# Strassen's sums built in the accumulation banks: a chain of products per bank instead of a bank per product

## The chip, the cores and the metric

The kernel runs on one core of a Trainium2 chip. The metric is the device time of one launch in microseconds, the median of the runs shown.

## What is computed

A two-layer decoder trunk on 1024 tokens of width 1024, in float32. Each sub-layer ends in `x <- LayerNorm(alpha * x + f(x))`. Layer 0 mixes with a gated linear recurrence and a convolution that share an output projection, layer 1 with pooling windows; both layers then attend to 256 memory tokens and pass a SwiGLU block of 2816 hidden channels.

```python
def memory_cross_attention(x, mem_n, w_q, w_k, w_v, w_o):
    ...
    s = jnp.einsum('bshd,bmhd->bhsm', q, k).astype(jnp.float32) * (XA_DH ** -0.5)
    p = jax.nn.softmax(s, axis=-1).astype(x.dtype)
    o = jnp.einsum('bhsm,bmhd->bshd', p, v).reshape(B, S, D_MODEL)
    return o @ w_o

def swiglu_ffn(x, w_gate, w_up, w_down):
    return (jax.nn.silu(x @ w_gate) * (x @ w_up)) @ w_down
```

## The kernel before

**Products.** A float32 product is made of three passes with float32r operands (`mm3`, lines 202 to 206): each operand is held as a high part (a cast on ScalarE, line 209) and a low part (the difference, line 210, on VectorE or GpSimd). The names `dh` and `dl` in the profile are these parts, `wp` and `raw` the loaded weights and hidden layer, `op` the parts of the gate and up stage, `D` and `P` the accumulation banks (512 floats on 128 partitions each; there are eight). A plain matmul here is 128 x 128 by 128 x 512.

**Seven products.** Most large products are taken as 2 x 2 blocks in Winograd's form of Strassen's scheme. With A in halves of its rows and of the inner dimension, and B in halves of the inner dimension and of its columns, it forms combinations S1 to S4 of A's blocks and T1 to T4 of B's, and then

```text
P1 = A11 B11   P2 = A12 B21   P3 = S4 B22   P4 = A22 T4   P5 = S1 T1   P6 = S2 T2   P7 = S3 T3
C11 = P1 + P2            C12 = P1 + P6 + P5 + P3
C21 = P1 + P6 + P7 + P4  C22 = P1 + P6 + P7 + P5
```

The function `seven` runs them for the output projection of the first mixer (once), the scores against the memory, the output of the attention (both in each layer) and the down projection (each layer). A product has four blocks of 128 tokens, each with its own bank; so a product takes four of the eight banks. It runs over pairs `g` of chunks of the inner dimension: two pairs in the attention stages (48 matmuls a product), six in the down projection, the last a single chunk (132 matmuls a product). For each pair it calls `hook` (loads, combinations, norms that are to stand there in each engine's list), prepares operands until `look(j)` pairs are ready ahead (`operands7`, through `down_B` for the weights' combinations, lines 762 to 786), and issues the matmuls for the four blocks. After a product `add` takes its four blocks. The last product of a stage goes block by block from the pair `outer` on. All engines run their lists in the order in which the program is written; a matmul waits for its bank until the tile that held it before was read for the last time.

**Sums before.** Each product starts its own banks. Sums that serve several blocks of C are made on VectorE: U = P1 + P6 (and + P7) in a tile `U` of SBUF, or several additions of the same bank to the residual rows `x` (`add_down`, `add_attn`, and `add` in the scores). In the down projection P5 and P7 are added twice per block, P6 goes into U and from there into three places, one of them on GpSimd. The orders are 1, 2, 6, 5, 3, 7, 4 in the attention stages (`ORDER_A`) and 1, 5, 7, 6, 4, 3, 2 in the down projection (`ORDER_D`).

**Gate and up.** `ffn` works on 20 pairs of chunks of the hidden layer per layer with the same scheme (order 1, 6, 2, 7, 5, 4, 3); here a product is 12 matmuls into one bank. P1 is copied to SBUF on ScalarE, and VectorE forms U2 = P1 + P6, U3 = U2 + P7 and U2 + P5 (lines 1311 to 1322); `finish` adds the last product to one of them and applies silu, or multiplies with the gate.

**Norms.** `add_res` (line 241) puts a bank on the residual; the last addition to a row half also gives the row sums (`acc`), from which `ln_a` and `ln_b` (lines 256 and 257) make the norm. In `ffn_down` the norms of blocks 4 to 7 (`norm_b`) are called in the hook of P3.

## Time and profile before

| | us |
|---|---|
| median of 3 runs (lowest, highest) | 2537.41 (2535.52, 2541.55) |
| span of the profiled execution | 2534.8 |
| time of the profiled execution | 2537.4 |
| TensorE busy | 2338.5 (92%) |
| VectorE busy | 2010.5 (79%) |
| ScalarE busy | 1009.6 (40%) |
| GpSimd busy | 1097.2 (43%) |

The span runs from the first to the last instruction of one execution. The page gives shares of the whole span; the stages differ, so the table of windows (a stretch of time, and how long each engine was busy in it) is read beside it. In a timeline row the first number is the start, the second the duration, and the brackets give how long the engine had been idle and which instruction ended the wait.

### The profile page before, as it was taken

Reading aid. Unit: us, or ns where it says so; the run is one execution under the profiler, and the core shown is the slowest. Engines: PE = TensorE matmul, PEld = TensorE weight load, DVE = VectorE, ACT = ScalarE, POOL = GpSimd, SP = SyncE. Lnnn points to the kernel's source line nnn. Section 1 sums busy time; section 2 is a strip of 40 time slices with the busy share of each in tenths; the row PEclk is TensorE's granted clock in tenths of the full one; section 3 lists DMA queues with packets and bytes.
Section 4 is the critical chain, followed back from the end, with each engine's and each line's share of the span. In section 5 each row is a group of like instructions: output and inputs, shape, how many; then the busy total and the mean of one; then the engine's idle time right before and its main releaser. Section 6 shows DMA issues by size and latency. Waiting matters only on the chain. (4 is left out here: it accounts for less than half of the span.)

```text
span 2534.8 us, 29436 instructions
## 1 busy us (share of the span) xinstructions
PE 2338.5 (92%) x11208; PEld 1927.8 (76%) x11208; DVE 2010.5 (79%) x2202; ACT 1009.6 (40%) x1647; POOL 1097.2 (43%) x601
## 2 busy tenths in 40 slices
PE   8999998898988999999887999798899999998987
PEld 6777777686867888888676789686688888876766
DVE  6986789988996777777888856899867777778777
ACT  3255554353636323223232444455552322332342
POOL 2332447776581212212754674567511121237464
PEclk9999999898999999999998999899999999999989
DMA  4211133140202323323733343202122332356332
GB/s 179 67 34 34 34 118 124 59 167 9 100 26 92 107 81 115 115 83 129 273 117 130 107 159 101 91 17 108 51 77 90 116 116 80 116 191 224 112 110 98
DMA packets 84476, 263.26 MB, mean 104 GB/s; under 512 B 8432, under 2 KB 8944, under 8 KB 84336
## 3 DMA queue, kind: packets, MB, share of 16 engines
q1 hardware_dynamic: 58464, 203.97, 23.4%
q10 hardware_dynamic: 25872, 57.42, 6.4%
q8 instruction: 88, 1.44, 0.2%
q14 instruction: 52, 0.43, 0.1%
HBM read 198.97 MB, written 62.39 MB: 103 GB/s over the span
## 5 line engine op out<-in xcount | busy, mean ns | idle before, releaser
L204 PE MATMUL D<-dh,dl 128*128 128x512 f32 x1176 | 476.2, 405 | 87.4 <-POOL dl L210 52.1
L205 PE MATMUL D<-dl,dh 128*128 128x512 f32 x1176 | 477.0, 406 | 56.4 <-DVE dl L210 56.3
L206 PE MATMUL D<-dh,dh 128*128 128x512 f32 x1176 | 472.1, 401 | 0.0
L205 PE MATMUL P<-xl,op 128*128 128x512 f32 x1120 | 435.7, 389 | 0.0
L204 PE MATMUL P<-xh,op 128*128 128x512 f32 x1120 | 435.7, 389 | 0.0
L206 PE MATMUL P<-xh,op 128*128 128x512 f32 x1120 | 435.7, 389 | 0.0
L204 PEld LDWEIGHTS D<-dh,dl 128*128 128x128 f32 x1176 | 229.9, 196 | 145.9 <-POOL dl L210 57.7
L1199 POOL TENSOR_TENSOR s<-hf,hf 128x512 f32<-128x512 f32 x22 | 35.7, 1622 | 659.4 <-PE P L206 560.8
L205 PEld LDWEIGHTS D<-dl,dh 128*128 128x128 f32 x1176 | 230.3, 196 | 117.4 <-DVE dl L210 69.7
L210 POOL TENSOR_TENSOR dl<-raw,dh 128x1024 fp32r<-128x1024 f32 x84 | 230.0, 2751 | 185.8 <-ACT dh L209 167.0
L206 PEld LDWEIGHTS D<-dh,dh 128*128 128x128 f32 x1176 | 229.7, 195 | 48.2
L205 PEld LDWEIGHTS P<-xl,op 128*128 128x128 f32 x1120 | 210.2, 188 | 43.8
L204 PEld LDWEIGHTS P<-xh,op 128*128 128x128 f32 x1120 | 210.2, 188 | 43.7
L206 PEld LDWEIGHTS P<-xh,op 128*128 128x128 f32 x1120 | 210.2, 188 | 43.5
L119 POOL TENSOR_TENSOR wl<-raw,wh 128x1024 fp32r<-128x1024 f32 x64 | 173.0, 2716 | 160.1 <-ACT wh L117 150.4
L210 DVE TENSOR_TENSOR dl<-wp,dh 128x1024 fp32r<-128x1024 f32 x96 | 172.2, 1803 | 75.5 <-ACT dh L209 65.0
L1153 DVE TENSOR_TENSOR op<-raw,op 128x512 fp32r<-128x512 f32 x200 | 151.4, 757 | 87.5 <-ACT op L1152 71.6
L1152 ACT CAST op<-raw 128x512 fp32r<-128x512 f32 x200 | 120.4, 618 | 204.8 <-DVE raw L1179 123.4
L209 ACT CAST dh<-wp 128x1024 fp32r<-128x1024 f32 x96 | 94.8, 988 | 254.4 <-DVE wp L770 65.6
L359 DVE SCALAR_TENSOR_TENSOR cacc<-sig,par,cacc 128x1023 f32<-128x1023 f32 (+14 forms) x120 | 177.5, 1479 | 2.5
L210 POOL TENSOR_TENSOR dl<-xf,dh 128x1024 fp32r<-128x1024 f32 x48 | 148.6, 3118 | 32.1 <-ACT dh L209 31.9
L210 DVE TENSOR_TENSOR dl<-B,dh 128x1024 fp32r<-128x1024 f32 x48 | 121.8, 2563 | 24.9 <-ACT dh L209 24.9
(283 smaller groups left out, 4879.1 us busy)
## 6 DMA issues: line engine op xcount, KB each, us to landing
raw<-hD SPq DMA_DIRECT2D x70, 512.0 KB, 3.4
raw<-in_wg SPq DMA_DIRECT2D x44, 512.0 KB, 3.9
raw<-in_wu SPq DMA_DIRECT2D x44, 512.0 KB, 3.3
hD<-s ACTq DMA_DIRECT2D x44, 512.0 KB, 4.8
wp<-in_wd SPq DMA_DIRECT2D x40, 512.0 KB, 5.0
xD<-x ACTq DMA_DIRECT2D x32, 512.0 KB, 4.0
x<-xD SPq DMA_DIRECT2D x32, 512.0 KB, 5.7
raw<-in_w_in SPq DMA_DIRECT2D x23, 512.0 KB, 3.4
```

The costliest lines, as they stand in the source:

```text
L119: eng.tensor_tensor(lo, raw, hi.bitcast(F32), op=ALU.subtract)
L204: mm(out, ll, rh, start=start, stop=False)
L205: mm(out, lh, rl, start=False, stop=False)
L206: mm(out, lh, rh, start=False, stop=stop)
L209: self.nc.scalar.copy(hi, src)
L210: getattr(self.nc, lo_engine).tensor_tensor(lo, src, hi.bitcast(F32), op=ALU.subtract)
L359: nc.vector.scalar_tensor_tensor(acc[:, s:], u[:, :S - s], w[:, j:j + 1], acc[:, s:], op0=ALU.mult, op1=ALU.add)
L1152: nc.scalar.copy(pg[:, 0], src)
L1153: getattr(nc, lo_engine).tensor_tensor(pg[:, 1], src, pg[:, 0].bitcast(F32), op=ALU.subtract)
L1199: gp(s1, a21, a22, op=ALU.add)
```

## The change

P6, P7 and P4 accumulate on in the four banks of P1, and P3 in those of P5 (`CHAIN`): the first matmul of such a product doesn't start the bank anew. So the banks of P1 hold P1, then P1 + P6, then P1 + P6 + P7, and last C21 complete; those of P5 hold P5, then P5 + P3. After each product of a chain its sum of so far is read where C needs it: C11 takes the bank after P1 and the bank of P2, C12 the bank after P6 and the bank after P3, C22 the bank after P7 and the bank after P5, C21 the bank after P4. The U tiles and the additions to them go. As a bank must not be written on before the sum of so far is read, the products' orders change, so that between two products of a chain another one stands, with the exception of P4 after P7 in `seven`: 1, 2, 5, 6, 3, 7, 4 (`ORDER_A`), 1, 5, 6, 3, 7, 4, 2 (`ORDER_D`), 1, 2, 6, 5, 7, 3, 4 (`ORDER_P`). With the orders some hooks move: the last combinations in the attention stages to the first pair of P6, the loads of `x` to P2 and P5, the norms of blocks 4 to 7 in the down projection from P3 to P2, and six pairs of operands are made ahead under P4 and P2 instead of P3 and P2.

```diff
+ORDER_A = (1, 2, 5, 6, 3, 7, 4)
+ORDER_D = (1, 5, 6, 3, 7, 4, 2)
+ORDER_P = (1, 2, 6, 5, 7, 3, 4)
+CHAIN = {1: 1, 6: 1, 7: 1, 4: 1, 5: 5, 3: 5, 2: 2}
+ENDS = (4, 3, 2)
...
-        def mm(bank, o, p, g):
+        def mm(bank, o, p, g, j):
             tk = slice(p * P, (p + 1) * P)
             for i in range(o[0].shape[1]):
                 c = 2 * g + i
-                self.mm3(bank, o[0][:, i, tk], o[1][:, i, tk], o[2][:, i, :], o[3][:, i, :], c == 0, c == nc - 1)
-
+                self.mm3(bank, o[0][:, i, tk], o[1][:, i, tk], o[2][:, i, :], o[3][:, i, :], c == 0 and j == CHAIN[j], c == nc - 1,
+                         j != CHAIN[j])
+
+        chains = {}
         for j in order:
-            banks = [self.ps(f"D{j}") for _ in range(4)]
             hold = []
             for g in range(ng):
                 hook(j, g)
+                if g == 0:
+                    if j == CHAIN[j]:
+                        chains[j] = [self.ps(f"D{j}") for _ in range(4)]
+                    banks = chains[CHAIN[j]]
...
-    def add_down(self, j, b, x0, x1, s0, s1, u):
...
-        elif j == 5:
-            self.add_res(x0, b, 1)
-            self.add_res(x1, b, 1)
-        elif j == 7:
-            self.add_res(x1, b, 0)
-            self.add_res(x1, b, 1, first=False)
-        elif j == 6:
-            nc.vector.tensor_tensor(u, b, u, op=ALU.add)
-            for x, eh, eng in ((x0, 1, nc.gpsimd), (x1, 0, nc.vector)):
-                sl = x[:, eh * 512:eh * 512 + 512]
-                eng.tensor_tensor(sl, sl, u, op=ALU.add)
-            self.add_res(x1, u, 1, first=False, acc=s1)
...
+    def add_block(self, j, b, x0, x1, s0, s1):
+        x, st, eh, first = {1: (x0, None, 0, True), 2: (x0, s0, 0, False), 6: (x0, None, 1, True), 3: (x0, s0, 1, False),
+                            5: (x1, None, 1, True), 7: (x1, s1, 1, False), 4: (x1, s1, 0, True)}[j]
+        self.add_res(x, b, eh, first=first, acc=st)
...
+            q, eh = {1: (p, 0), 2: (p, 0), 6: (p, 1), 3: (p, 1), 5: (p + 4, 1), 7: (p + 4, 1), 4: (p + 4, 0)}[j]
+            if j in (2, 3, 7):
+                tt(half(q, eh), b, half(q, eh), op=ALU.add)
             else:
-                tt(half(p + 4, 0), b, half(p + 4, 0), op=ALU.add)
+                nc.scalar.copy(half(q, eh), b)
...
             elif j == 7:
-                B22[g], r = take(), T3.pop(g)
-                tt(r, B22[g], r, op=ALU.subtract)
+                r = T3.pop(g)
+                tt(r, B22.pop(g), r, op=ALU.subtract)
             elif j == 6:
-                r = T[g]
+                B22[g], r = take(), T[g]
                 tt(r, B22[g], r, op=ALU.subtract)
...
-            b = self.ps(f"P{j}")
-            product(b, w, X[j])
+            if j == CHAIN[j]:
+                banks[j] = self.ps(f"P{j}")
+            b = banks[CHAIN[j]]
+            product(b, w, X[j], j == CHAIN[j])
...
-            if j == 1:
-                p1 = self.t2("p1", [512])
-                nc.scalar.copy(p1, b)
-            elif j == 6:
-                u2 = self.t2("u2", [512])
-                tt(u2, b, p1, op=ALU.add)
+            if j in (1, 6, 5):
+                u[j] = self.t2("u", [512])
+                nc.scalar.copy(u[j], b)
             elif j == 2:
-                finish(m, st, 0, 0, p1, b)
+                finish(m, st, 0, 0, u.pop(1), b)
             elif j == 7:
-                u3 = self.t2("u3", [512])
-                tt(u3, b, u2, op=ALU.add)
-            elif j == 5:
-                finish(m, st, 1, 1, u3, b)
-                tt(u2, b, u2, op=ALU.add)
-            elif j == 4:
-                finish(m, st, 1, 0, u3, b)
+                finish(m, st, 1, 1, u.pop(5), b)
+            elif j == 3:
+                finish(m, st, 0, 1, u.pop(6), b)
             else:
-                finish(m, st, 0, 1, u2, b)
+                finish(m, st, 1, 0, None, b)
...
-            if j == 3 and 1 <= g < 5:
+            if j == 2 and 1 <= g < 5:
                 norm_b(3 + g)
 
-        self.seven(ORDER_D, self.down_made, self.down_ops, len(self.hD), HF, lambda j: 6 if j in (3, 2) else 4, add, hook, 1)
+        self.seven(ORDER_D, self.down_made, self.down_ops, len(self.hD), HF, lambda j: 6 if j in (4, 2) else 4, add, hook, 1)
```

Three places show how the lists of the engines move. The first is VectorE's list in the first down projection, before, at the end of the block of additions that follows P6 (`U` is the tile of the sums, `x` the residual, `wp` a weight block that becomes a combination, `dl` a low part):

```order
L241 SCALAR_TENSOR_TENSOR x_9719,lst_9611<-x_9719,U_9614 128x512
L846 TENSOR_TENSOR U_9614<-D_1636_10327,U_9614 128x512
L849 TENSOR_TENSOR x_9764<-x_9764,U_9614 128x512
L241 SCALAR_TENSOR_TENSOR x_9764,lst_9612<-x_9764,U_9614 128x512
L779 TENSOR_TENSOR wp_1528_9629<-wp_1660_10507,wp_1528_9629 128x1024
L210 TENSOR_TENSOR dl_10566<-wp_1528_9629,dh_10565 128x1024
```

and after, at the additions that follow P7, the product ahead of P4 (line 247 is `add_res`, 786 the combination for P4, 216 the split):

```order
L247 SCALAR_TENSOR_TENSOR x_9449,lst_9382<-x_9449,D_1383_9396 128x512
L247 SCALAR_TENSOR_TENSOR x_9489,lst_9383<-x_9489,D_1384_9397 128x512
L247 SCALAR_TENSOR_TENSOR x_9534,lst_9384<-x_9534,D_1385_9398 128x512
L786 TENSOR_TENSOR wp_1386_9399<-wp_1534_10453,wp_1386_9399 128x1024
L216 TENSOR_TENSOR dl_10496<-wp_1386_9399,dh_10495 128x1024
```

Of a product's block nothing is left but one addition from the bank, and the next combination stands right behind the fourth.

The second place is TensorE's list in the first attention output, before, in the product after P2 (which is P6), from its first block of tokens to its second, with the waits:

```order
L204 MATMUL D_947_5881<-dh_5817,dl_5814 128x512
L205 MATMUL D_947_5881<-dl_5818,dh_5813 128x512
L206 MATMUL D_947_5881<-dh_5817,dh_5813 128x512
L204 MATMUL D_948_5882<-dh_5817,dl_5814 128x512
L205 MATMUL D_948_5882<-dl_5818,dh_5813 128x512
L206 MATMUL D_948_5882<-dh_5817,dh_5813 128x512
```

and after, where the product behind P2 is P5:

```order
L210 MATMUL D_907_5813<-dh_5741,dl_5738 128x512
L211 MATMUL D_907_5813<-dl_5742,dh_5737 128x512
L212 MATMUL D_907_5813<-dh_5741,dh_5737 128x512
L210 MATMUL D_908_5814<-dh_5741,dl_5738 128x512 [waits DVE_49]
L211 MATMUL D_908_5814<-dl_5742,dh_5737 128x512
L212 MATMUL D_908_5814<-dh_5741,dh_5737 128x512
```

Every block now waits for VectorE, which must have read the block of P2 whose bank it takes.

The third place is ScalarE's list in the gate and up stage of the first layer, in one round, before (`p` is the copy of P1):

```order
L1152 CAST op_8882<-raw_8671 128x512 [waits DMAHW1_49,DMAHW0_49,DVE_49]
L1311 COPY p_1401_8900<-P_1400_8887 128x512 [waits PE_49]
L1152 CAST op_8902<-s_8822 128x512 [waits DMAHW2_49]
L1152 CAST op_8920<-raw_8671 128x512 [waits Activation_49]
L1152 CAST op_8939<-raw_8534 128x512 [waits DVE_49,Activation_49]
```

and after (`u` is the copy of a sum from a bank):

```order
L1274 COPY u_8567<-P_1264_8552 128x512 [waits PE_49]
L1112 CAST op_8570<-raw_8351 128x512 [waits DMAHW5_49,DVE_49]
L1178 ACTIVATE sg_8550<-sg_8550 128x512 [waits DVE_49]
L1112 CAST op_8589<-raw_8212 128x512 [waits DVE_49,Activation_49]
L1274 COPY u_8604<-P_1264_8552 128x512 [waits PE_49]
```

Copies of the bank's sums after P1 and after P6 now stand among the casts of the operands.

## Rows read from the trace of the kernel before

**Rows 1.** The page, engine table: busy us, share of the span, instructions.
```profile
PE 2338.5 (92%) x11208; PEld 1927.8 (76%) x11208; DVE 2010.5 (79%) x2202; ACT 1009.6 (40%) x1647; POOL 1097.2 (43%) x601
```

**Rows 2.** Waits of TensorE by releaser: us in total, times, longest us.
```profile
PE D L205 <- DVE dl L210: 56.3, 27, 12.7
PE D L204 <- POOL dl L210: 52.1, 12, 9.6
PE D L204 <- ACT dh L209: 35.2, 11, 11.1
```

**Rows 3.** Windows by stage: from:to, us, busy PE, PEld, DVE, ACT, POOL, clock, DMA.
```profile
392.00:490.00 98.00, 82.68 (x346) 66.41 (x346) 95.69 (x76) 38.07 (x51) 82.63 (x36) 0.93 0.19 67
...
833.00:1214.00 381.00, 381.00 (x1682) 315.48 (x1682) 278.31 (x399) 118.93 (x203) 71.59 (x42) 1.00 0.34 113
1214.00:1475.00 261.00, 226.37 (x926) 180.23 (x925) 217.77 (x158) 87.89 (x102) 161.66 (x71) 0.93 0.43 150
```

**Rows 4.** Windows by product of the first down projection: P7, P6, P4, P3, P2.
```profile
1292.10:1328.50 36.40, 32.88 (x134) 25.99 (x134) 28.44 (x23) 13.13 (x14) 16.47 (x7) 0.95 0.30 99
1328.50:1361.80 33.30, 30.97 (x134) 24.59 (x133) 26.59 (x21) 11.15 (x12) 15.72 (x7) 1.00 0.37 131
1361.80:1405.80 44.00, 32.52 (x133) 25.86 (x132) 37.00 (x28) 13.88 (x15) 24.31 (x12) 0.84 0.39 132
1405.80:1435.70 29.90, 29.90 (x134) 24.75 (x133) 25.01 (x21) 16.13 (x21) 23.36 (x15) 1.00 0.35 109
1435.70:1475.20 39.50, 33.67 (x135) 26.64 (x134) 32.46 (x33) 12.23 (x16) 23.41 (x12) 0.87 0.36 117
```

**Rows 5.** Timeline before and in P4, VectorE and TensorE: start, us, engine, line, [idle before].
```profile
1356.57 1.22 DVE L779 TENSOR_TENSOR wp<-wp,wp 128x1024 f32<-128x1024 f32 x1
...
1366.81 3.42 DVE L779 TENSOR_TENSOR wp<-wp,wp 128x1024 f32<-128x1024 f32 x1
1371.50 1.23 DVE L210 TENSOR_TENSOR dl<-wp,dh 128x1024 fp32r<-128x1024 f32 x1 [1.26 <-ACT dh L209]
1372.65 0.68 DVE L846 TENSOR_TENSOR U<-D,U 128x512 f32<-128x512 f32 x1
...
1373.97 1.78 DVE L241 SCALAR_TENSOR_TENSOR x<-x,U 128x512 f32<-128x512 f32 x1
...
1384.73 3.35 DVE L779 TENSOR_TENSOR wp<-wp,wp 128x1024 f32<-128x1024 f32 x1
...
1389.38 0.77 PE L204 MATMUL D<-dh,dl 128*128 128x512 f32 x1 [11.09 <-ACT dh L209]
```

**Rows 6.** Gate and up stage: one group of lines (count, busy, mean ns), two timeline rows.
```profile
L1314 DVE TENSOR_TENSOR u<-P,p 128x512 f32<-128x512 f32 x40 | 27.4, 684 | 12.4 <-PE P L206 12.4
...
1018.44 0.69 DVE L1224 TENSOR_TENSOR hf<-P,u 128x512 f32<-128x512 f32 x1 [0.79 <-PE P L206]
...
1023.08 0.69 DVE L1224 TENSOR_TENSOR hf<-P,u 128x512 f32<-128x512 f32 x1
```

**Rows 7.** Timeline in P2: first layer on TensorE, second layer on ScalarE.
```profile
1446.82 0.79 PE L205 MATMUL D<-dl,dh 128*128 128x512 f32 x1 [3.97 <-DVE dl L210]
...
2486.63 1.06 ACT L209 CAST dh<-raw 128x1024 fp32r<-128x1024 f32 x1 [8.66 <-DMA raw<-hD]
```

**Rows 8.** Timeline of the first attention output: product after P2, P2's first addition, the transposes.
```profile
714.38 0.39 PE L204 MATMUL D<-dh,dl 128*128 128x512 f32 x1
...
717.62 0.68 DVE L241 SCALAR_TENSOR_TENSOR x<-x,D 128x512 f32<-128x512 f32 x1
...
775.49 1.41 PE L266 MATMUL xt<-kc,x 128*128 128x128 f32 x8 [4.34 <-DVE U L874]
```

**Rows 9.** Timeline of the mixer output: P7's first reading, and the next stage's start.
```profile
485.57 0.68 DVE L874 TENSOR_TENSOR U<-D,U 128x512 f32<-128x512 f32 x1
...
501.42 0.58 PE L204 MATMUL pk<-wh,wl 128*128 128x256 f32 x1 [5.71 <-POOL wl L119]
```

**Rows 10.** Timeline of the first scores: the first reading of P2's sums.
```profile
592.32 0.69 DVE L1000 TENSOR_TENSOR p<-D,U 128x512 f32<-128x512 f32 x1 [6.34 <-PE D L206]
```

More of the change, by code (lines that the diff above doesn't have):

```diff
@@ L199, in drain, with mm3 @@
             self.pump()
-    def mm3(self, out, lh, ll, rh, rl, start, stop):
+    def mm3(self, out, lh, ll, rh, rl, start, stop, more=False):
         mm = self.nc.tensor.matmul
-        mm(out, ll, rh, start=start, stop=False)
-        mm(out, lh, rl, start=False, stop=False)
-        mm(out, lh, rh, start=False, stop=stop)
+        mm(out, ll, rh, start=start, stop=False, skip_group_check=more)
+        mm(out, lh, rl, start=False, stop=False, skip_group_check=more)
+        mm(out, lh, rh, start=False, stop=stop, skip_group_check=more)
     def split(self, hi, lo, src, lo_engine="vector"):
@@ L586, in mixer0_out @@
         sts = [self.sm("lst", 5) for _ in range(NT)]
-        U = [self.t2("U", [512]) for _ in range(4)]
         A, B = self.sides
@@ L596, in add @@
         def add(j, p, b):
-            self.add_attn(j, b, x[p], x[p + 4], sts[p], sts[p + 4], U[p])
+            self.add_block(j, b, x[p], x[p + 4], sts[p], sts[p + 4])
             if j == 3:
@@ L624, in hook @@
                 self.combos_B(B, 2, nc.gpsimd)
-            if j == 6:
-                load(4 + 2 * g)
-                load(5 + 2 * g)
-                if g == 1:
-                    self.combos_B(B, 3, nc.vector)
-                    self.combos_A(A, 3, nc.gpsimd)
+            if (j, g) in ((2, 1), (5, 0)):
+                load(4 + 2 * (j == 5))
+                load(5 + 2 * (j == 5))
+            if j == 6 and g == 0:
+                self.combos_B(B, 3, nc.vector)
+                self.combos_A(A, 3, nc.gpsimd)
             if j == 7:
@@ L780, in get @@
             elif j == 3:
-                r = B22.pop(g)
+                r = B22[g]
             else:
@@ L825, in seven @@
                 for p in range(4):
-                    mm(banks[p], o, p, g)
+                    mm(banks[p], o, p, g, j)
                     self.pump()
@@ L995, in add @@
         def add(j, p, b):
[L996 to L1010 removed]
+            q, eh = {1: (p, 0), 2: (p, 0), 6: (p, 1), 3: (p, 1), 5: (p + 4, 1), 7: (p + 4, 1), 4: (p + 4, 0)}[j]
+            if j in (2, 3, 7):
+                tt(half(q, eh), b, half(q, eh), op=ALU.add)
             else:
[L1012 removed]
+                nc.scalar.copy(half(q, eh), b)
         def hook(j, g):
[L1015 removed]
+            if j == 6 and g == 0:
                 self.combos_B(B, 3, nc.vector)
@@ L1082, in attn_out @@
         sts = [self.sm("lst", 6) for _ in range(NT)]
-        U = [self.t2("U", [512]) for _ in range(4)]
         self.w.lo_engine = ("gpsimd",)
@@ L1088, in add @@
                 self.ffn_first_half(layer)
-            self.add_attn(j, b, x[p], x[p + 4], sts[p], sts[p + 4], U[p])
+            self.add_block(j, b, x[p], x[p + 4], sts[p], sts[p + 4])
             if j == 3:
@@ L1106, in hook @@
                 self.combos_B(B, 2, nc.vector)
-            if j == 6:
-                for t in (4 + 2 * g, 5 + 2 * g):
+            if (j, g) in ((2, 1), (5, 0)):
+                for t in (4 + 2 * (j == 5), 5 + 2 * (j == 5)):
                     x[t] = self.page("x", [D])
                     nc.sync.dma_start(x[t], self.xD[t])
-                if g == 1:
-                    self.combos_B(B, 3, nc.vector)
-                    self.combos_A(A, 3, nc.gpsimd)
+            if j == 6 and g == 0:
+                self.combos_B(B, 3, nc.vector)
+                self.combos_A(A, 3, nc.gpsimd)
             if j in (7, 4):
@@ L1185, in operands, with product @@
                 yield operand(src[j], lo_engine)
-        def product(bank, w, x):
+        def product(bank, w, x, first):
             for k in range(4):
-                self.mm3(bank, w[k][0], w[k][1], x[k][0], x[k][1], k == 0, k == 3)
+                self.mm3(bank, w[k][0], w[k][1], x[k][0], x[k][1], k == 0 and first, k == 3, not first)
         later = self.later
@@ L1277, in ffn @@
         self.w.split_ahead = 0
-        order = (1, 6, 2, 7, 5, 4, 3)
+        order = ORDER_P
         def all_ops():
@@ L1294, in ffn @@
         self.down_made = []
+        banks, u = {}, {}
         for n, (m, j) in enumerate(stream):
@@ L1349, in ffn_down @@
         sts = [self.sm("lst", 5) for _ in range(NT)]
-        U = [self.page("U", [2, 512]) for _ in range(2)]
         gb, gx = [], []
@@ L1360, in add @@
                 norm_b(p - 1)
-            self.add_down(j, b, x[p], x[p + 4], sts[p], sts[p + 4], U[p // 2][:, p % 2, :] if U else None)
-            if j == 6 and p == 3:
-                U.clear()
+            self.add_block(j, b, x[p], x[p + 4], sts[p], sts[p + 4])
             if j == 4:
```

59 lines of the change are left out of this document (7 added, 52 removed).

## Prediction

> **What bounds the kernel now.** I read the engine table first [rows 1]: TensorE is busy for 2338.5 of 2534.8 us, so all that a change of this kind can win is the 196 us in which TensorE does nothing, plus what a lower clock costs around such gaps. The table of waits [rows 2] says who ends those gaps: the operands of the products called D, that is the splits of line 210 and the casts of line 209 (56.3 + 52.1 + 35.2 us). The windows by stage [rows 3] put them in their places: the gate and up stage (833 to 1214) has TensorE busy for 381.00 of 381.00 us at full clock. Nothing can be won there, only lost. The down projection has 226.37 of 261.00 and the mixer output 82.68 of 98.
>
> The down projection decides. Cut by product [rows 4] (132 matmuls each), P3 takes 29.90 us with TensorE busy all the time: that is the floor. P7 takes 36.4, P6 33.3, P4 44.0 and P2 39.5. These five take 183.1 us where 5 × 29.9 = 149.5 would do: 33.6 us of excess in each layer.
>
> Where P4's 14 us come from [rows 5]: VectorE makes each operand of P7, P6 and P4 by a combination (3.42 us beside GpSimd's work; 1.22 in the first row, the first of P4), ScalarE casts it, VectorE splits it (1.23): from 1366.81 to the split's end at 1372.73 about 5.85 us a pair of chunks, where TensorE needs 29.9/5.5 = 5.44. So the supply has no reserve, and whatever VectorE does in between makes TensorE's next operand late. After P6 that is the U block: from 1372.65 to 1384.73, 12.1 us for four blocks of tokens (for each, U from the bank 0.68, an addition to one x and one to the other, this with both inputs in SBUF 1.78). Only then comes the next combination, and TensorE waits 11.09 us.
>
> **The change, part by part.** *Gate and up.* Per round VectorE loses four operations (seven readings of the banks become three), ScalarE gains two copies. The removed additions cost 0.684 us each [rows 6]; a copy I put at the same, as an estimate. VectorE goes from 278 to 278 − 80 × 0.684 = 224 us a layer, ScalarE from 119 to 119 + 40 × 0.684 = 146, both of 381. TensorE is full already, so this is worth 0. The new price is a handover: P6, P7, P4 and P3 may start only when the bank's last sum has been read, 4 × 20 × 2 = 160 times. In each case one other product lies between, 12 matmuls of 381.00/1682 = 0.2265 us, so 2.72 us, against a reading of 0.68. The reader may thus come 2.0 us late for nothing. How late VectorE comes now [rows 6]: the reading at 1018.44 had waited 0.79 for its product, so it was on time; the next product ended 2.72 later, at 1021.16, and its reading stands at 1023.08, 1.9 us late. That is close, but with four operations fewer in a round it gets shorter. I take 0, from 0 to +6.
>
> *Down projection.* The U block goes: four additions after each product, about 4 × 0.68 = 2.7 us. GpSimd's additions and ScalarE's copies go with it, which were beside other work. I run the new order (P1, P5, P6, P3, P7, P4, P2) from 1292.1 on, where P5 ends; up to there all stays. P6 takes P7's place: 36.4 less the four additions of P5 that go, 2.7, makes 33.7. P3 needs no combinations: 29.9. P7's first operands are made under P3: 29.9. Under P7 VectorE has P3's additions (2.7) and, of P7 and P4, 5.5 pairs of combinations at 5.85 (32.2), together 34.9: P7's first addition comes 5 us after P7's end, and P4, the only product whose bank's last sum is the product right before it, waits for it: 5.0 + 0.7. Behind such a wait the clock is lower: P4's window of before exceeds 29.9 + 11.5 of waits by 2.6 at a granted clock of 0.84 [rows 4]; I take half, 1.3. Under P4 VectorE has 2.7 + 2.5 × 5.85 + five plain splits of 1.2 to 2.5, at most 30: no further wait. P4: 36.9. P2's splits of before stood behind the norms of four blocks, and TensorE waited 3.97 for one; in the last layer these norms also send their results out through SP's queue, in which P2's loads stood behind them: a cast waited 8.66 us for one [rows 7]. Now splits and loads come first; I give P2 31.5, for norms that end late. Sum: 33.7 + 29.9 + 29.9 + 36.9 + 31.5 = 161.9 against 183.1: **−21 us in each layer, −42 in both.** If the combinations run at 1.22 instead of 3.42, P4 has no wait: −27. If P7 is as slow as it was and the norms hold up the end by 4 more: −10.
>
> *Attention output, twice.* P7's U block goes, and with it the transposes' wait of 4.34 for it [rows 8]. Against it: all eight banks are taken when P2 ends, so P5 waits for VectorE's reading of P2. The product behind P2 started at 714.38, and the first addition of P2 ran from 717.62 to 718.30 [rows 8]: +3.9. That is −0.4; with somewhat shorter waits for splits behind it, since it starts later, −1 each; from −5 (the splits come sooner) to +5. *Mixer output.* P4 may start only after the first reading of P7, now at 485.57 behind norms; 48 matmuls of 0.2265 from 486.3 on end at 497. But the next stage has TensorE idle for 5.71 us until 501.42, for a split on GpSimd [rows 9] at the end of VectorE's and ScalarE's lists, and VectorE has 12 additions fewer. I take 0, from −3 to +6. *Scores, twice.* VectorE had waited 6.34 us for P2's sums [rows 10]: such a reading is on time. Copies on ScalarE I count like it, without a row. 0, from −1 to +3.
>
> Sum: −42 − 2 + 0 + 0 + 0 = −44. The profiled execution lies 2.6 us above its span, at 2537.4, which is the median too: **2493 us.** The good ends of all unknown costs: −54 − 10 − 3 − 2 = −69, giving 2468; the bad ends: −20 + 10 + 6 + 6 + 6 = +8, if all came at once.
>
> **Rivals.** *The banks take the place of the operands.* In the five attention stages (mixer output, two scores, two outputs) P2 to P5 and P7 to P4 are ten handovers that stand behind whatever VectorE has queued. For it: the readings at 717.62 and 485.57 were late [rows 8, 9], and VectorE is busy for 95.69 of 98 us in the mixer output. At 5 us for each it would be 50; the waits that stand elsewhere in these stages take up part of that, and with half of it, 25, the time is about 2518 (2505 to 2530). The new gaps cost clock as well: P4's window with its 11 us wait was granted 0.84 in the mean, where 1.00 is 2.4 GHz and the lower level, 1.2, is 0.50. The Trainium skill, "TensorE: Matmul & The Clock Gate", section "A second HAM failure mode: psum-queue depth-cycling", reports a kernel in which cycling through PSUM banks left small idle gaps between groups, over which the clock went up and down; by that rule this rival would be the likely one. Against it: the scores' readings are on time, and the worst gap, P4's, is counted already.
>
> *The operand chain is the bound, not what stands in it.* With 5.85 against 5.44 a pair, P6, P7 and P4 may run no faster than their combinations; what VectorE wins goes into splits that it then does earlier, for nothing. P7 and P6 stay at 36 and 33, P4 keeps a wait of 8 to 10, and the sum is −8 to 0: about 2533. The Trainium skill, "SBUF — State Buffer", section "Who interferes with whom", says that a VectorE operation with two SBUF inputs contends with GpSimd's reads and one with a single SBUF input does not; by that rule the combinations keep their 3.4 us, since GpSimd's splits stay, and only the additions get cheap. The rows agree: 0.68 from a bank, 1.78 from SBUF. Against the rival: 12.1 us of U block went with 11.09 us of waiting, nearly one for one.
>
> *Slower: the gate and up stage.* ScalarE copies three sums a round, in a queue in which a copy that waits for its product holds the casts behind it, and a cast that waits for VectorE holds the copy. The stage has no spare time, so every reading more than 2.0 us late is paid in full, 160 times. It decides from 44/160 = 0.28 us each; at 0.6 us it is +96 − 44, about 2589. For it: a reading of before was 1.9 us late. Against it: both engines are idle for a good part of each round, and VectorE has fewer readings.
>
> **How the numbers follow.** Forecast (2470 to 2508) 0.62; banks 0.18; chain 0.09; slower 0.11. The likeliest gives 2493. The range, 2470 to 2530, leaves out the slower case and most of the chain's. Faster by over 0.2% (5 us, about what a measurement of this kernel can tell from no change): 0.62 + 0.17 + 0.02 of the chain's = 0.81. Within: 0.08. Slower: 0.11.
>
> **What would show it.** In the changed profile: the wait of 11 us at P4 for line 209's cast is gone, and one of about 5 us for an addition of VectorE stands at P4's start; P3 and P7 take about 30 us, P2 about 31; in the gate and up stage TensorE is busy for 381 of 381 us and VectorE for about 224; the transposes' wait for U is gone; P5 of the attention output starts after a wait of about 4 us for an addition. If the gate and up stage is longer than 383 us, the third rival is at work; if P6 and P7 stay above 33 us, the second; if the ten handovers cost over 20 us in sum, the first.

## The result

The changed kernel takes 2483.55 us (median of 4 runs, 2480.97 to 2486.67), the kernel before in the same comparison 2537.86 (4 runs): a ratio of 0.9783, 95% interval 0.9769 to 0.9797, or 54 us less. The profiled execution, the slowest of the four, took 2486.67 with a span of 2484.9. Beside the span of before, 2534.8, this is 49.9 less, though the stretch ahead of the mixer's output projection, in code that is the same in both, is 3.1 longer; between executions that stretch differs by as much. Of the 49.9, TensorE's idle time makes up 37.1 (196.3 to 159.2) and its busy time 12.8, for the same number of matmuls; the mean granted clock is 0.974 in place of 0.968.

The engine table, against [rows 1] (busy us, share, instructions):

```profile
PE 2325.7 (94%) x11208; PEld 1920.4 (77%) x11208; DVE 1842.3 (74%) x1950; ACT 1050.7 (42%) x1723; POOL 1044.8 (42%) x573
```

VectorE lost 252 instructions and 168 us; TensorE issues as many matmuls as before. Its waits, against [rows 2] (us, times, longest; the lines are now 210, 215 and 216):

```profile
PE D L210 <- DVE x L247: 39.1, 8, 14.8
PE D L211 <- DVE dl L216: 31.8, 13, 10.5
PE D L210 <- POOL dl L216: 22.9, 5, 9.6
PE D L210 <- ACT dh L215: 13.5, 8, 3.5
PE pk L210 <- POOL wl L125: 7.4, 2, 4.6
```

The waits for operands fell from 143.6 to 68.2 us. A kind that was not there has come, `D` waiting for `x` of line 247: a product waits until VectorE has read the bank that it is to write. Two of these eight waits, both in the mixer output, are most of the 39.1. The two kinds together are 107.3 us, 36.3 less than the operands' waits of before.

Windows by stage (mixer output, gate and up, first down projection; busy PE, PEld, DVE, ACT, POOL, clock, DMA), against [rows 3]:

```profile
395.90:504.70 108.80, 80.59 (x339) 65.26 (x339) 92.35 (x85) 40.19 (x53) 78.83 (x37) 0.87 0.18 63
827.50:1210.50 383.00, 381.82 (x1682) 315.29 (x1681) 245.35 (x320) 140.77 (x243) 71.48 (x42) 1.00 0.33 113
1210.40:1443.70 233.30, 218.46 (x925) 175.50 (x923) 192.58 (x134) 83.81 (x96) 147.50 (x64) 0.98 0.45 159
```

The gate and up stage now runs from 827.5 to 1210.5, 383.0 us where it was 381.0.

By stages, from a stage's first D matmul on TensorE to its last, and what lies between (us; both layers where there are two):

| | before | after | difference |
|---|---|---|---|
| start to mixer output | 392.8 | 395.9 | +3.1 |
| mixer output, with what follows it up to the first scores | 164.1 | 164.8 | +0.7 |
| scores | 93.8, 93.7 | 90.4, 91.7 | −3.4, −2.0 |
| scores to attention output | 29.8, 29.8 | 30.9, 30.9 | +1.1, +1.1 |
| attention output | 105.9, 105.8 | 98.6, 99.6 | −7.3, −6.2 |
| attention output to down (gate and up) | 427.7, 427.7 | 429.8, 429.7 | +2.1, +2.0 |
| down projection | 261.1, 260.6 | 233.3, 233.7 | −27.8, −26.9 |
| down to the second layer's scores | 133.2 | 141.8 | **+8.6** |
| end of TensorE to end of span | 8.8 | 13.8 | **+5.0** |

The first down projection by product (P6, P3, P7, P4 with its wait, P2), against [rows 4]:

```profile
1285.60:1320.20 34.60, 31.66 (x134) 24.64 (x134) 26.42 (x18) 15.94 (x18) 16.67 (x7) 1.00 0.34 114
1320.20:1350.20 30.00, 30.00 (x134) 24.86 (x133) 26.43 (x16) 11.93 (x13) 22.51 (x9) 1.00 0.34 112
1350.20:1380.10 29.90, 29.90 (x133) 24.45 (x131) 23.05 (x21) 10.33 (x12) 15.60 (x6) 1.00 0.70 240
1380.10:1413.70 33.60, 31.70 (x134) 26.10 (x134) 29.19 (x21) 14.59 (x16) 22.35 (x8) 0.95 0.34 109
1413.70:1443.70 30.00, 30.00 (x133) 24.54 (x131) 22.00 (x30) 11.91 (x18) 13.07 (x15) 1.00 0.16 53
```

Three of five products are at the floor of 30 us with TensorE busy throughout; before it was one. Around the start of P4 (timeline, VectorE and TensorE), against [rows 5]:

```profile
1352.59 1.22 DVE L780 TENSOR_TENSOR wp<-wp,wp 128x1024 f32<-128x1024 f32 x1
...
1365.12 1.22 DVE L786 TENSOR_TENSOR wp<-wp,wp 128x1024 f32<-128x1024 f32 x1
...
1375.40 3.42 DVE L786 TENSOR_TENSOR wp<-wp,wp 128x1024 f32<-128x1024 f32 x1
1380.05 1.23 DVE L216 TENSOR_TENSOR dl<-wp,dh 128x1024 fp32r<-128x1024 f32 x1 [1.23 <-issue]
1381.20 0.68 DVE L247 SCALAR_TENSOR_TENSOR x<-x,D 128x512 f32<-128x512 f32 x1
...
1383.63 1.25 DVE L786 TENSOR_TENSOR wp<-wp,wp 128x1024 f32<-128x1024 f32 x1
...
1382.03 0.47 PE L210 MATMUL D<-dh,dl 128*128 128x512 f32 x1 [1.90 <-DVE x L247]
```

The block of 12.1 us is four additions, 1381.20 to 1383.63, and the wait of 11.09 is one of 1.90.

### The profile page after: what moved, and what is told of

It is laid out like the page before. It is cut to its first block, busy times and chain, and to the rows that moved or that the text cites. A ratio compares the mean times of both kernels' runs of the same rounds, so it can differ in the third digit from the quotient of the medians.

```text
span 2484.9 us, 29326 instructions
## 1 busy us (share of the span) xinstructions
PE 2325.7 (94%) x11208; PEld 1920.4 (77%) x11208; DVE 1842.3 (74%) x1950; ACT 1050.7 (42%) x1723; POOL 1044.8 (42%) x573
## 5 line engine op out<-in xcount | busy, mean ns | idle before, releaser
L210 PE MATMUL D<-dh,dl 128*128 128x512 f32 x1176 | 471.4, 401 | 75.6 <-DVE x L247 39.1
L211 PE MATMUL D<-dl,dh 128*128 128x512 f32 x1176 | 471.4, 401 | 32.1 <-DVE dl L216 31.8
L212 PE MATMUL D<-dh,dh 128*128 128x512 f32 x1176 | 467.1, 397 | 0.0
L1113 DVE TENSOR_TENSOR op<-raw,op 128x512 fp32r<-128x512 f32 x200 | 139.5, 698 | 166.5 <-ACT op L1112 163.7
L216 DVE TENSOR_TENSOR dl<-wp,dh 128x1024 fp32r<-128x1024 f32 x96 | 189.3, 1988 | 81.6 <-ACT dh L215 65.2
L216 POOL TENSOR_TENSOR dl<-xf,dh 128x1024 fp32r<-128x1024 f32 x48 | 141.5, 2964 | 39.7 <-ACT dh L215 29.2
```

What stands on the lines that cost most here:

```text
L210: mm(out, ll, rh, start=start, stop=False, skip_group_check=more)
L211: mm(out, lh, rl, start=False, stop=False, skip_group_check=more)
L212: mm(out, lh, rh, start=False, stop=stop, skip_group_check=more)
L216: getattr(self.nc, lo_engine).tensor_tensor(lo, src, hi.bitcast(F32), op=ALU.subtract)
L1113: getattr(nc, lo_engine).tensor_tensor(pg[:, 1], src, pg[:, 0].bitcast(F32), op=ALU.subtract)
```

## The experiments

The medians of before in the four sets of runs were 2538.78, 2537.88, 2538.24 and 2539.16 us; a ratio stands to the one of its own set. Each run has a short name, by which later parts refer to it.

**Which part brings what.** The change was cut in three, each added alone to the kernel before.

Run d1: the down projection alone (chains, order, norms, look-ahead); the other stages keep their banks and U sums:

```diff
-ORDER_D = (1, 5, 7, 6, 4, 3, 2)
+ORDER_D = (1, 5, 6, 3, 7, 4, 2)
...
-            self.add_down(j, b, x[p], x[p + 4], sts[p], sts[p + 4], U[p // 2][:, p % 2, :] if U else None)
...
+            self.add_block(j, b, x[p], x[p + 4], sts[p], sts[p + 4])
```

> The kernel before, changed in the down projection alone (chains, order 1, 5, 6, 3, 7, 4, 2, one addition per product and block, norms of blocks 4 to 7 under P2, six pairs ahead under P4 and P2). Theory: the gain is made in the down projection and each stage stands by itself. Between the traces of before and after the two down projections are 27.8 and 26.9 us shorter and what follows them is 8.6 and 5.0 longer, so -41, about 2497. Rival: the stages feed each other; the first product of the down projection, which got 5.8 us shorter though nothing in it was changed but its additions, lives on what the gate and up stage left ready. Then this kernel gains only about 30, 2508.

2496.14 us, 0.9833 (0.9818 to 0.9848), −42.6. The stage itself fell by 27.4 and 27.0 (233.7 and 233.6), more than the total: the stretch behind the first down projection is 9.4 longer than before (142.6), the tail (from TensorE's end to the end of the span) 5.0.

Run d2: gate and up alone:

```diff
-        order = (1, 6, 2, 7, 5, 4, 3)
+        order = ORDER_P
...
-            b = self.ps(f"P{j}")
+            if j == CHAIN[j]:
+                banks[j] = self.ps(f"P{j}")
+            b = banks[CHAIN[j]]
```

> The kernel before, changed in the gate and up stage alone. Theory: TensorE is full there, 160 handovers cost nothing: 2537, within 4 us. Rival: VectorE, with 55 us less work in each of these stages, makes the first operands of the down projection sooner: -8 to -12, about 2528. Third: handovers cost 0.1 us and more each, +16, 2554.

2538.39 us, 0.9997 (0.9988 to 1.0007): nothing in the sum. But the stage itself takes 383.1 us in each layer, 2.1 more than before. In the first down projection P1 gets 5.8 shorter (30.4 after 36.2), P5, which was 42.0, takes 44.2 and a wait of 1.3, and the stage falls by 2.2, the second one by 1.5. So two small effects cancel.

Run d3: mixer output, scores and attention output alone:

```diff
-ORDER_A = (1, 2, 6, 5, 3, 7, 4)
+ORDER_A = (1, 2, 5, 6, 3, 7, 4)
...
-            self.add_attn(j, b, x[p], x[p + 4], sts[p], sts[p + 4], U[p])
+            self.add_block(j, b, x[p], x[p + 4], sts[p], sts[p + 4])
```

> The kernel before, changed in the mixer output, the scores and the attention outputs alone (chains and order 1, 2, 5, 6, 3, 7, 4). Theory: the handovers from P2 to P5 and from P7 to P4 cost what they win in the mixer output (0 to +4), while the attention outputs win 7.3 and 6.2 and the scores 3.4 and 2.0 less about 1 each in what follows: -16, about 2522. Rival: the waits of 14.8 and 12.6 us that now stand in the mixer output are a net loss of 10 and more; then -6, 2532.

2522.77 us, 0.9933 (0.9918 to 0.9948), −16.0. So the parts are −42.6, −0.4 and −16.0, −59 together against −54 for all; the difference lies within the intervals.

**Sums or order?** Run d4: the down projection in the new order, with the norms and the look-ahead of the change, but each product in its own banks and U made on VectorE as before:

```diff
-ORDER_D = (1, 5, 7, 6, 4, 3, 2)
+ORDER_D = (1, 5, 6, 3, 7, 4, 2)
...
-            if j == 3 and 1 <= g < 5:
+            if j == 2 and 1 <= g < 5:
...
-        ..., lambda j: 6 if j in (3, 2) else 4, add, hook, 1)
+        ..., lambda j: 6 if j in (4, 2) else 4, add, hook, 1)
```

> The kernel before with the new order of the down projection (1, 5, 6, 3, 7, 4, 2, norms and look-ahead as in the changed kernel), but every product in its own banks and the sums made on VectorE as before (copy of P1, U, additions to x). It tells the order from the chains. Theory of the prediction: the additions on VectorE between two combinations are what TensorE waits for; then the order without the chains wins a third or less of what the down projection wins: -8 to -15, about 2525. Rival: P3, which needs no combinations, now stands behind P6 and covers the block of additions, so the order alone gives most of it: -30 and more, 2507 or less.

2532.16 us, 0.9972 (0.9962 to 0.9983), −6.6, a little less than the theory had. The stage takes 251.5 and 252.0. P7 and P4 are at 29.9 by the order alone; the U block after P6 now makes P3 late, and P2 waits as well (timeline, TensorE):

```profile
1351.18 0.50 PE L206 MATMUL D<-dh,dl 128*128 128x512 f32 x1 [3.37 <-POOL dl L212]
...
1447.15 0.79 PE L206 MATMUL D<-dh,dl 128*128 128x512 f32 x1 [6.67 <-POOL dl L212]
```

The chains take another 36 us off (2532.16 to 2496.14): the sums carry the win, the order by itself is a small part. The reverse, run o2, chains with the old place of P3:

```diff
-ORDER_D = (1, 5, 6, 3, 7, 4, 2)
+ORDER_D = (1, 5, 6, 7, 4, 3, 2)
...
-            if j == 2 and 1 <= g < 5:
+            if j == 3 and 1 <= g < 5:
...
-        ..., lambda j: 6 if j in (4, 2) else 4, add, hook, 1)
+        ..., lambda j: 6 if j in (3, 2) else 4, add, hook, 1)
```

> The changed kernel with the old place of P3 in the down projection: 1, 5, 6, 7, 4, 3, 2, so that P7 stands right behind P6 and P4 right behind P7 in the same banks (two adjacent handovers a layer in place of one; norms and the six pairs ahead under P3 and P2 as before). If a handover waits for VectorE, which under P6 and under P7 has four additions and 5.5 combinations of 5.85 us (34.9) for a product of 29.9: P7 and P4 wait about 5 each, against 1.9 in the changed kernel: +8 a layer, about 2500 us (2495 to 2506). If the sums' additions were all of the gain and the order is nothing: 2484 to 2487.

2496.09 us, 0.9837 (0.9822 to 0.9852). The total is as expected, 12.5 above the changed kernel, but not by that way. There is one wait, not two, and it is twice the size (timeline, VectorE and TensorE):

```profile
1324.98 3.36 DVE L780 TENSOR_TENSOR wp<-wp,wp 128x1024 f32<-128x1024 f32 x1
1329.79 1.23 DVE L216 TENSOR_TENSOR dl<-wp,dh 128x1024 fp32r<-128x1024 f32 x1 [1.44 <-ACT dh L215]
1330.93 0.68 DVE L247 SCALAR_TENSOR_TENSOR x<-x,D 128x512 f32<-128x512 f32 x1
...
1331.76 0.77 PE L210 MATMUL D<-dh,dl 128*128 128x512 f32 x1 [11.79 <-DVE x L247]
```

P6's reading stands behind combinations and splits for P7, and P7 waits for it. In these 11.79 us VectorE catches up, so that P4 doesn't wait at all. Each layer's stage is 13.2 and 13.1 longer than in the changed kernel, yet 8.2 come back in the stretch behind the first layer (133.6) and 5.0 in the tail (8.8): the two lengths of the kernel before. This pointed to the norms, which stand under P3 here and under P2 in the change. Run d4, which has them under P2 and no chains, says the same: 142.0 and 14.3. And with the chains in place the order is worth 12.5 us, about twice what it is worth without them.

**Is it VectorE's time?** Run u6: eight additions of a scratch tile, behind P6's additions; they touch no bank:

```diff
+            if j == 6 and p == 3:
+                for _ in range(8):
+                    nc.vector.tensor_tensor(dm, dm, dm, op=ALU.add)
```

> The changed kernel with a block of VectorE work put back in the down projection: eight additions of a scratch tile 128 x 512 (both inputs in SBUF, 1.2 to 1.8 us each, about 12 us like the old U block), behind P6's four additions; no bank is read by them. If VectorE's time between two combinations is what TensorE waits for, one for one, as the prediction argued from 12.1 us of U block and 11.09 us of waiting: +12 a layer, 2508 us. If P3, which needs no combination, covers part of it (VectorE is idle for about 9 us between P6's end and P7's end in the changed kernel, and the wait of 1.90 at P4 grows by what is left): +3 to +6 a layer, 2490 to 2496. If it was the bank's several readings, or the additions on GpSimd, and not VectorE's time: 2484 to 2486.

Run u7, the same behind P7's:

```diff
+            if j == 7 and p == 3:
```

> The same block of eight scratch additions, but behind P7's four additions, straight ahead of P4's next combination, where the old U block stood in the kernel before. One for one: +12 a layer, 2508 us, with a wait of 10 us or more in P4. With three pairs of P4 made ahead (16 us) against a block of 12 and a combination with cast and split of 5.85: a wait of 3 to 6 in P4, and norms that end later, together +4 to +8 a layer, 2492 to 2500. If VectorE's time isn't it: 2484 to 2486.

2493.38 us (0.9826, 0.9812 to 0.9841) and 2493.66 (0.9828, 0.9813 to 0.9842): +10 in each. First u6, then u7 (timeline, VectorE and TensorE):

```profile
1327.46 11.05 DVE L1324 TENSOR_TENSOR dm<-dm 128x512 f32<-128x512 f32 x8
...
1339.71 0.50 PE L211 MATMUL D<-dl,dh 128*128 128x512 f32 x1 [3.43 <-DVE dl L216]
...
1386.95 0.76 PE L210 MATMUL D<-dh,dl 128*128 128x512 f32 x1 [3.66 <-DVE x L247]
```

```profile
1382.03 5.81 DVE L1324 TENSOR_TENSOR dm<-dm 128x512 f32<-128x512 f32 x8
...
1401.60 15.96 DVE L216 TENSOR_TENSOR dl<-wp,dh 128x1024 fp32r<-128x1024 f32 x5 [1.26 <-ACT dh L215]
...
1425.70 0.62 PE L210 MATMUL D<-dh,dl 128*128 128x512 f32 x1 [2.56 <-POOL dl L216]
```

VectorE's time between operands counts, without any bank or U tile in it. But not one for one: 11.05 us cost 6.6 and 6.1 of a layer's stage (P3 waits 3.43, P4 3.66 in place of 1.90), and 5.81 cost 4.6 and 4.3. The wait at P4 stays at 1.89; the 4.6 and 4.3 come out only in P2, a product and more later, at the first operand that has no reserve left.

**The price of a handover.** Run p1: P6 right behind P1 in the gate and up stage:

```diff
-ORDER_P = (1, 2, 6, 5, 7, 3, 4)
+ORDER_P = (1, 6, 2, 5, 7, 3, 4)
```

> The changed kernel with P6 right behind P1 in the gate and up stage (1, 6, 2, 5, 7, 3, 4): 40 adjacent handovers in both layers, each waiting for ScalarE's copy of P1 from the bank. If TensorE must stand still until the copy has ended: at least 0.7 us of copy and the signals' way, 1.0 to 1.5 us each, +40 to +60: 2524 to 2545 us, and more (2565) where the copy stands behind casts. If a bank can be written on while it is read, or the copy is hidden: 2484 to 2488.

2528.43 us, 0.9961 (0.9947 to 0.9975): 44.9 more than the changed kernel, for 40 handovers 1.1 us each. The stage is 22.2 longer; 15.5 of that are waits, and TensorE's busy time for the same matmuls is 6.7 longer (388.56 after 381.82). Waits of TensorE in the first layer's stage (us, times, longest), first the changed kernel, then this one:

```profile
PE P L210 <- ACT u L1274: 0.7, 1, 0.7
PE P L210 <- DVE hf L1184: 0.4, 1, 0.4
```

```profile
PE P L210 <- ACT u L1274: 16.2, 20, 3.4
```

Nineteen of the twenty waits are 0.68 us, the first is 3.4. With another product between, these two short waits are all that the 80 handovers of a layer leave, and the stage is 2.0 longer than before.

**What gave back 13.6 us?** In the changed kernel the first norm of blocks 4 to 7 begins behind P2's last split, and P2's first addition only after all four (timeline, VectorE; then the next stage's wait on TensorE):

```profile
1420.41 1.58 DVE L216 TENSOR_TENSOR dl<-wp,dh 128x512 fp32r<-128x512 f32 x1 [3.68 <-ACT dh L215]
1421.91 1.27 DVE L262 SCALAR_TENSOR_TENSOR x<-x,lst,lng 128x1024 f32<-128x1024 f32 x1
...
1431.04 1.28 DVE L263 SCALAR_TENSOR_TENSOR x<-x,lst,lnb 128x1024 f32<-128x1024 f32 x1
1432.24 0.68 DVE L247 SCALAR_TENSOR_TENSOR x<-x,D 128x512 f32<-128x512 f32 x1
...
1452.98 0.68 DVE L247 SCALAR_TENSOR_TENSOR x<-x,D 128x512 f32<-128x512 f32 x1
...
1458.68 0.58 PE L210 MATMUL pk<-wh,wl 128*128 128x256 f32 x1 [4.64 <-POOL wl L125]
```

P2's last matmul ended at 1443.7; its last addition runs 9.3 later, where before it was 2.4 (1477.59 after 1475.2). Four kernels went after this and after the two long waits of the mixer output. Run c1 moves norms and next weights forward:

```diff
-        ..., lambda j: 6 if j in (4, 2) else 4, add, hook, 1)
+        ..., lambda j: {4: 7, 2: 6}.get(j, 4), add, hook, 1)
...
-                if layer < DEPTH - 1 and p < 2:
-                    self.w.ahead(2 * p + 2, 2 * p + 4)
...
                 norm_b(3 + g)
+                if layer < DEPTH - 1 and g > 2:
+                    self.w.ahead(2 * g - 4, 2 * g - 2)
```

> The changed kernel with two moves in the down projection: seven pairs of operands are made ahead under P4 (before: six), so that P2's last split no longer stands behind P4's additions and norms and the norms of blocks 4 to 7 can begin as soon as P4 has ended; and the casts and splits of the next stage's first weights stand among those norms instead of behind the first two blocks of P2. If late norms are what gave back part of the win (P2's first addition came 7 us after its product, the tail grew from 8.8 to 13.8 us, the next weights' splits were 2.8 and 4.6 late): the tail back to 9 or 10, the two waits gone, 2472 to 2477 us. If the next stage is bound by something else, for example VectorE's or GpSimd's total of work there: only the tail, 2479 to 2481; if the splits among the norms slow the norms (3.4 instead of 1.3 us beside GpSimd): no gain, 2482 to 2486.

2479.63 us, 0.9765 (0.9752 to 0.9779): 4 less than the changed kernel, within the intervals of both. The tail is 11.2 in place of 13.8, but the two waits of the next stage only became one of 8.65. The last addition of P2 still ran 8.7 after its product (1448.64 after 1439.9). So the early splits were not the point. Run c2 takes the two long waits of the mixer output:

```diff
-                for i in range(3):
-                    self.combos_A(A, i, nc.vector)
+                self.combos_A(A, 0, nc.vector)
                 self.combos_B(B, 2, nc.gpsimd)
+            if j == 5 and g == 0:
+                for i in (1, 2):
+                    self.combos_A(A, i, nc.vector)
...
-            if j == 7:
+            if j == 4:
                 self.ln_b(x[2 * g], sts[2 * g], gb)
```

> The changed kernel with two moves in the mixer's output projection: the combinations S3 and S2 (11 us of VectorE) stand ahead of P5's first matmuls in the list and behind the reading of P2, not ahead of that reading; and the norms of blocks 0 to 3 stand behind the readings of P7, not ahead of them. If the two waits there (14.8 at P5, 12.6 at P4) are plain loss of TensorE's time: both mostly gone, the stage 15 us or more shorter, 2466 to 2470 us. If VectorE's total of work sets the end of the stage (95.6 us busy in 112.7) and the waits only move: 2480 to 2485. In between, one of the two is won, 2473 to 2479: I expect this, since P6's operands need S2 and will now be late.

2479.00 us, 0.9762 (0.9749 to 0.9775). The two waits, of the changed kernel and then of this one (timeline, VectorE and TensorE):

```profile
424.40 4.49 DVE L741 TENSOR_TENSOR y<-y,y 128x1024 f32<-128x1024 f32 x2
...
434.06 0.77 PE L210 MATMUL D<-dh,dl 128*128 128x512 f32 x1 [14.80 <-DVE x L247]
...
488.01 3.17 DVE L263 SCALAR_TENSOR_TENSOR x<-x,lst,lnb 128x1024 f32<-128x1024 f32 x1
...
491.94 0.76 PE L210 MATMUL D<-dh,dl 128*128 128x512 f32 x1 [12.55 <-DVE x L247]
```

```profile
422.12 0.76 PE L210 MATMUL D<-dh,dl 128*128 128x512 f32 x1 [6.00 <-DVE x L247]
...
470.21 0.47 PE L210 MATMUL D<-dh,dl 128*128 128x512 f32 x1 [1.42 <-DVE x L247]
```

The stage is 20.0 shorter (88.8), and the stretch up to the scores, which begins with the next weights' splits, 13.4 longer (69.4 after 56.0). Of 20 us of waiting that went, 6.6 were TensorE's to win. I had expected one wait to go and one to stay; the first fell to 6.00 and the second to 1.42, and the gain was as if one had gone.

Run c4: both sets together, and T3 behind P2's readings in the attention output:

```diff
-            if j == 2 and g == 0:
+            if j == 5 and g == 0:
                 self.combos_B(B, 2, nc.vector)
```

> Both sets of moves together, and in the attention's output the combination T3 behind the readings of P2 (before: ahead of them; P5 waited 3.3 and 4.3 us for those readings). If the parts add up: the sum of what the other two win against 2483.5, and 3 to 7 more: 2460 to 2472 us. If the T3 combination only moves the wait into P5 or P6: the sum of the two, without more.

2469.82 us, 0.9729 (0.9716 to 0.9742): the sum of the two (−4 and −4.5) and 5 more. P5 of the attention output doesn't wait now, P3 waits 2.26 and 3.32 instead, and the stage is 97.7 and 97.5 long after 98.6 and 99.6. That is 3.0 of the 5. The two down projections, which have nothing new against c1, are 1.7 and 2.1 shorter than there: P4, behind the same wait (1.86 after 1.89), takes 30.0 us in the first layer where it took 31.7. Its window, in c1 and in c4:

```profile
1378.20:1409.90 31.70, 31.70 (x133) 26.03 (x134) 26.90 (x17) 14.15 (x16) 21.73 (x8) 0.95 0.34 112
```

```profile
1371.20:1401.30 30.10, 30.06 (x133) 24.91 (x134) 25.68 (x17) 13.79 (x15) 21.61 (x8) 1.00 0.34 114
```

So the granted clock behind a wait of 1.9 us was 0.95 in one kernel and 1.00 in another; what decides it no run here shows. Last, run c5, P2's additions ahead of the norms of the block before:

```diff
-            if j == 2 and p:
-                norm_b(p - 1)
             self.add_block(j, b, x[p], x[p + 4], sts[p], sts[p + 4])
...
                 self.ln_a(x[p], sts[p])
+                if p:
+                    norm_b(p - 1)
```

> The kernel with all moves so far (c4_all), and in the last product of the down projection each block of P2 is added to the residual before the norm of the block ahead of it is issued, not behind it. In c4_all the additions of P2 are 5.5 us apart although the products have long ended, because VectorE stands still behind each addition for ScalarE's squares and GpSimd's root (1.37 and 0.72 us) before it takes the next; the last square holds the cast of the next stage's third weight page, and TensorE waits 10.2 us for it. If this chain of addition, square, root, norm is what gives back the win: that wait is gone or below 3, the tail after TensorE's end falls from 12.7 to about 9 us, together 9 to 13 us: 2457 to 2461 us. If GpSimd's splits of the weights themselves are the limit: only the tail, 2466 to 2468; if nothing: 2469 to 2471.

2460.86 us, 0.9691 (0.9678 to 0.9704): 9 less than the kernel ahead of it, and faster than both kernels of this case, by 78 and 23 us. The cast that stands behind the last square, and the next stage's wait, in c4 and in c5 (timeline, ScalarE and TensorE):

```profile
1443.82 1.03 ACT L123 CAST wh<-raw 128x1024 fp32r<-128x1024 f32 x1
...
1447.33 0.58 PE L210 MATMUL pk<-wh,wl 128*128 128x256 f32 x1 [10.22 <-POOL wl L125]
```

```profile
1437.98 1.03 ACT L123 CAST wh<-raw 128x1024 fp32r<-128x1024 f32 x1
...
1443.18 0.58 PE L210 MATMUL pk<-wh,wl 128*128 128x256 f32 x1 [4.40 <-POOL wl L125]
```

The tail is 9.7 in place of 12.7, the stretch behind the first layer 136.3 in place of 141.9. That is the 9 us. The additions, each of which waited for the norm of the block ahead, held the squares on ScalarE, these the cast of the next weights, and this GpSimd's split. The wait was to be gone or below 3; what is left of it, 4.40, was not taken further.

## Why the prediction was right, and where it was not

The forecast was −44 and the change is −54; 2483.55 lies 9.5 us under the 2493 and well inside the forecast case. The mechanism was the right one, some terms were not. What came on top of the forecast is in the attention outputs and the scores.

**Gate and up, 0.** It was +2.0 in each layer (383.0 us), inside the 0 to +6. That stands at the mark of 383 which I had set for the third rival, but at 0.025 us a handover it is a tenth of the 0.28 at which that rival decides. The handovers are nearly free because a product lies between, as p1 shows. What the stage lost, the next one gave back (d2). VectorE fell to 245, not 224: two kinds of the combinations that are left now take 24.6 and 21.9 us after 13.6 and 13.1, half of them beside GpSimd's sums (last section). That cost TensorE nothing that the waits show, as VectorE has room there.

**Down projection, −21 a layer.** Within the stage it was −27.8 and −26.9; 25.0 of that are in the five products (158.1 after 183.1). The rest is in P1 and P5, which I had left as they were; with gate and up alone (d2) P1 is as much shorter, and with the down projection alone (d1) it is not. P6 came out at 34.6 (33.7 forecast), P3 and P7 at 30.0 and 29.9 as forecast, P4 at 33.6, not 36.9. The failing term is VectorE's load under P7: I took every pair of combinations at 5.85 us, and two that began with GpSimd idle ran at 1.22, the rows at 1352.59 and 1365.12. From 1352.59 to 1381.20 the 5.5 pairs took 28.6 us, not 32.2, with the additions 31.0 and not 34.9. So the wait was 1.90, not 5.7. The clock's term, 1.3, measured 1.7 (31.7 us at a granted clock of 0.95 behind the wait, for 30.0); in c4 and c5 it was not there, behind the same wait. The sequence itself (a wait for an addition at P4, none in P3 and P7) is what the trace shows. P2 came out at 30.0, not 31.5.

**What came behind it I didn't count.** The norms that move to P2 were priced at 1.6 us in P2. They cost nothing there, but 8.6 in the next stage and 5.0 in the tail. I had followed the norms up to TensorE's last matmul and not to who waits for P2's additions: the squares, the casts behind them, the next weights. With these the down projection is worth −27.8 + 8.6 = −19.2 in the first layer and −26.9 + 5.0 = −21.9 in the second, −41.1 against −42. The sum was right because two errors cancel, which is luck.

**Attention output, −1 each.** It was −7.3 and −6.2. P5 waits 3.33 and 4.30 for P2's reading, and 3.9 was the forecast; the transposes' wait of 4.34 is gone. What I left out are other waits for operands, 2.34 in P5 and 2.27 in P4, and a granted clock of 0.87 over P4 and the transposes, which took 25.8 us and take 15.2 now at 1.00 (windows, before and after):

```profile
760.60:786.40 25.80, 18.59 (x82) 15.13 (x81) 22.16 (x32) 16.91 (x21) 9.88 (x8) 0.87 0.33 123
```

```profile
765.40:780.60 15.20, 15.15 (x81) 12.65 (x82) 9.85 (x19) 12.50 (x16) 4.70 (x2) 1.00 0.57 209
```

**Scores, 0:** −3.4 and −2.0. 2.2 of each is a wait in P2 that is 10.54 us, not 12.72; the two combinations ahead of its split take 2.35 us with GpSimd done, 4.50 before. Why GpSimd is done earlier there no run shows; the stage has not yet written on a bank a second time at that point, so this part is luck. Against it stand +1.1 in each layer behind the scores, where TensorE waits 1.07 for a copy by ScalarE, which has P4's four copies ahead of it now: the copies on ScalarE were the term that I had counted without a row. Together these stretches are the −16 of d3; the forecast had −2 for them.

**Mixer output, 0.** Right in the sum (+0.7), for the reason given: the time that the stage got longer (11.6) came back where the next stage had waited 5.71 and more [rows 9]. The wait at P4 is 12.55; the one at P5, 14.80, behind six combinations and two splits on VectorE, was not in the working at all.

**The first rival** (banks in place of operands) was given a sign, 20 us for the ten handovers, and by the sign it would be at work: the four in the mixer output and the attention outputs that wait add up to 35 us. In the mixer output it is what happened: waits for operands fell from 15.3 us to 0.9 there, and 27.3 us of waits at banks came. But the sign was wrong as a measure of the price. Where VectorE is behind, a wait at a bank stands in for a wait that TensorE would have had elsewhere, and d3 was faster by 16 us all the same; c2 took 20 us of them away and won 4.5. The granted clock fell in the mixer output, from 0.93 to 0.87, and rose in the mean of the whole span, from 0.968 to 0.974. The rule on idle gaps between groups that the prediction cites (the Trainium skill, "TensorE: Matmul & The Clock Gate", section "A second HAM failure mode: psum-queue depth-cycling") thus agrees with that one stage and did not set the time. **The second rival** (the operand chain is the bound) holds in P6 alone, at 34.6 with a wait of 1.80; d4 and u6 say that it is what stands in the chain. But what I held against it, 12.1 us of block for 11.09 of wait, nearly one for one, was too strong: in u6 11.05 us cost 6.6, in u7 5.81 cost 4.6.

## What to carry to other kernels

When an engine that prepares operands has no reserve, what it does between two of them counts even where its busy share is 79%, and sums that the accumulation banks can hold are nearly free on TensorE if another product lies between two that share a bank and the reader is not behind (2.0 us for 80 of them); adjacent, a handover costs the reading, its signals and all that the reader has queued before it. Price a moved block to the last one who waits for it, in the next stage too, not to the end of the stage. And the length of a wait is no measure of what its removal brings: undo it alone, and look at the start of the next stage.

## What the runs showed of the hardware

The same VectorE instruction took very different times with GpSimd beside it. In the first layer's gate and up stage a combination of `raw` had 682 ns in the kernel before and has this now (group of lines, mean ns of one):

```profile
L1136 DVE TENSOR_TENSOR raw<-raw,raw 128x512 f32<-128x512 f32 x20 | 24.6, 1229 | 0.0
```

The mean is made of ten that take 1.77 us, each beside GpSimd's sums of the hidden layer for 1.2 us and more, and ten that take 0.68 with GpSimd idle. Before, GpSimd was busy for about 0.4 us at the end of ten of the twenty, and none took longer for it.

The eight scratch additions took 5.81 us where GpSimd was idle, and 11.05 where it was busy for 6.37 of 10.9 us. Five plain splits on VectorE, both inputs in SBUF, took 15.96 us beside GpSimd, 3.2 each, against 1.23 for one alone. So a block of VectorE work has no price of its own; it has one for each neighbour.
